# Hybrid decoder layer: value projection moved between features six and seven, half of the rotary sine multiplies on GpSimd, and a new written order

## The chip, the cores and the metric

The kernel runs on one core of a Trainium2 chip. The metric is the device time of one execution in microseconds; the time before is the median of three runs. The engines are TensorE (PE in the profile; its weight loads PEld), VectorE (DVE), ScalarE (ACT), GpSimd (POOL) and SyncE (SP), which issues most loads.

## The reference

One decoder layer for 512 positions of width 1024, in float32:

```python
proj = x @ w_in
rq, rk, rv, rg, aq, ak, av, iq, ik, iw = jnp.split(proj, IN_SPLITS, axis=-1)
...
# rotary embedding of rq, rk, aq, ak, iq, ik
return jnp.concatenate([x1 * cos - x2 * sin, x1 * sin + x2 * cos], axis=-1)
...
# retention, 4 heads, chunks of 128
scores = jnp.einsum('nbhid,nbhjd->nbhij', qc, kc) * decay_intra
inner = jnp.einsum('nbhij,nbhjd->nbhid', scores, vc)
...
# indexer: 8 heads score all earlier keys, the 128 best are kept per query
score = jnp.einsum('bqh,bqhs->bqs', wb, logits)
_, sel = lax.top_k(score, topk)
# sparse softmax attention over the kept keys, 4 heads of 128
```

The retention output is normalised per head and multiplied by silu(rg); both outputs go through one output projection, a residual and a layer norm, then a SwiGLU feed-forward part of width 2816 with its own residual and norm.

## The kernel before, in words

**Products.** The projections are taken as three matmuls in the rounded float32 format (`mm3`, lines L101 to L103): high times high, high times low, low times high. So each half of a weight tile (128 x 1024) must be *prepared*: a high part `wh` and a low part `wl = raw - wh`. The number behind `wh` and `wl` counts the halves in the order in which TensorE uses them. The string `HOW` says how each half is prepared. For `V`, ScalarE casts (L93) and VectorE subtracts (L98). For `Q` (`lower`, L733 and L734), ScalarE copies `-raw` rounded into `wl` and a DMA issued by GpSimd adds `raw` to it in place; TensorE may use it when that DMA has landed. `N` is ScalarE with a VectorE operation of two scalars. Raw tiles of 1 MB come by SyncE into three buffers (`raw`).

**Main stream.** `main()` yields groups of TensorE work in this order: the eight features `pf0` to `pf7` (two halves each, 24 matmuls a half; 0 and 1 are attention keys, 2 and 3 attention queries, 4 and 5 retention keys `rkT`, 6 and 7 retention queries `rqT`), the retention value `pt1` in two parts (48 matmuls each; the second part stands inside `proj_pair`), and `proj_pair`: the attention value and the gate `grg` by a Strassen-like scheme of seven products P1 to P7, in the banks `pa`, `pc` and `pb`. Sums of raw tiles that this scheme needs (B11 + B12 and so on) are made by DMAs that add DRAM data to a raw tile (`plus`, L208). Then the mixed output projection (`mx`).

**Rotation.** `rope` (L273 to L278) takes two half copies on ScalarE (`rt2`), a cosine multiply on VectorE (L275), a sine multiply on VectorE (L276) and an addition on GpSimd (L278, L411). The index queries and the index key are rotated too; their sums go into `qs` and `ks` on VectorE. A rotated attention key or query leaves by a DMA into `akT` or `aqT`.

**Order.** Nothing is scheduled automatically: each engine takes its instructions in program order, and that is written by hand in `PLAN`. Its words: `M` is the next group of the main stream, `k` the next step of the side work (index rotation, index logits `lg`, top-k), `w` prepares the next half, `f` fetches a raw tile; `S1` to `S4`, `P3`, `P5` to `P7` make the sides of the Strassen scheme, `a`, `b`, `c`, `d` its raw sums, `kt`, `sc`, `st`, `oa`, `ob`, `rs`, `rg`, `tu` the steps of retention (`rs` scores on TensorE, `ri` outputs, `rz` turned outputs), `g` the gate's silu, `as`, `t`, `p` those of attention, `kl` the low part of the attention key (`akl`). A step that waits on one engine holds everything behind it on that engine. The feed-forward part, from about 268 us on, has an order of its own.

Of the kernel before, what the change touches and what calls it, by code (L numbers as in the profile page):

```python
# [53 lines left out]
def hybrid_layer_kernel(ctx: ExitStack, tc: tile.TileContext, xT, x, pos, w0, wf, wt, wo,  # L54
# [181 lines left out]
    for kt in range(KT):  # L236
# [30 lines left out]
        if kt in (3, 5):  # L267
            next(tables_it)
    def rope(dst, src, ct, st, lo=0):
        t1 = tmp("rt1")  # L270
# [2 lines left out]
        A.copy(t2[0:64, n], src[64:128, n])  # L273
# [1 line left out]
        V.tensor_tensor(t1[:, n], src[:, n], ct[:, n], op=ALU.mult)  # L275
        V.tensor_tensor(t2[:, n], t2[:, n], st[:, n], op=ALU.mult)  # L276
# [130 lines left out]
    def put_feature(c, i, acc):  # L407
        dst = feats[c // 2][:, 2 * (c % 2) + i]
        if c < 4:
            t1, t2 = rope(None, acc, CT, ST)  # L410
            G.tensor_tensor(t1, t1, t2, op=ALU.add)  # L411
# [587 lines left out]
w f M k M M w M M M M M M w k f M M k k w k M k w k M M M k M M M w M k M k M k M k k k f w w M k k k M M k k k M k k k f k M k f k k k M k k k M w k  # L999
# [891 lines left out]
```

## Time and profile before

| | us |
|---|---|
| median of three runs (604.88 to 606.65) | 605.32 |
| the profiled execution | 605.22 |
| its span | 603.4 |
| TensorE busy | 593.0 (98%) |
| VectorE busy | 528.6 (88%) |
| ScalarE busy | 399.4 (66%) |
| GpSimd busy | 200.3 (33%) |
| DMA: accumulating and other GpSimd queue, share of 16 engines | 41.2% |
| DMA: SyncE's loads, share of 16 engines | 37.8% |

The granted clock is 1.00 in all stretches shown. A row of the time line gives start and duration in us, then engine, line, operation, output and inputs, and in brackets the engine's idle time before it with what ended it. A row of waits gives the total, the number of times and the longest.

### The profile page before, as it was taken

The page shows a single profiled execution, that of the slowest core. Times are in us where ns is not written, and L with a number is a line of the kernel's source. Part 1 is how long each engine was busy: PE and PEld are TensorE (multiplying, and loading weights), DVE is VectorE, ACT ScalarE, POOL GpSimd, SP SyncE. Part 2 cuts the span into 40 slices and gives each one's busy share as a digit, 9 for nine tenths or more (in the row PEclk, how much of TensorE's full clock was granted, in tenths as well). Part 3 has the DMA queues.
Part 4 walks back from the last instruction along what each step waited for, and adds up shares of the span by engine and source line. Part 5 has one row for each costly group of instructions (what it writes and reads, how often), then busy time and mean ns, then how long its engine had stood idle before and what let it go on. Part 6 is the DMA issues. An engine that isn't in the chain of part 4 may idle for free.

```text
span 603.4 us, 9333 instructions
## 1 busy us (share of the span) xinstructions
PE 593.0 (98%) x3205; PEld 513.6 (85%) x3205; DVE 528.6 (88%) x941; ACT 399.4 (66%) x701; POOL 200.3 (33%) x220
## 2 busy tenths in 40 slices
PE   8999999999999999999999999999999999999996
PEld 6987888888887788889998888888888888888885
DVE  5868889988889999889999898989898989799995
ACT  4588575653689877677758677777677756485701
POOL 0067523351448021242003444444443423331120
PEclk9999999999999999999999999999999999999999
DMA  8988729989989698797347888888888999999412
GB/s 265 267 226 232 272 92 256 241 195 239 160 183 243 202 255 360 211 225 142 88 143 191 179 207 171 206 166 205 168 208 179 198 272 223 225 201 275 130 53 87
DMA packets 53600, 121.27 MB, mean 201 GB/s; under 512 B 9217, under 2 KB 26177, under 8 KB 48049
## 3 DMA queue, kind: packets, MB, share of 16 engines
q0 software_dynamic: 26160, 43.20, 41.2%
q1 hardware_dynamic: 26800, 76.69, 37.8%
q10 hardware_dynamic: 592, 0.79, 0.4%
q8 instruction: 25, 0.41, 0.3%
q14 instruction: 23, 0.18, 0.1%
HBM read 83.43 MB, written 2.10 MB: 142 GB/s over the span
## 4 chain that ended last, share of the span: by engine, by line
PE 85%; DMA 6%; POOL 3%; DVE 2%; issue 2%; SPq 2%; ACT 1%; POOLq 0%; ACTq 0%
PE ga L1098 17%; PE gc L1098 8%; PE gb L1098 4%; PE ga L1111 4%; PE pf L103 3%; PE pf L102 3%; PE pf L101 3%; DMA wl<-raw 3%; PE mx L101 2%; PE mx L103 2%; PE mx L102 2%; PE dl L101 2%; PE dl L103 2%; PE dl L102 2%; PE gc L1111 2%; DMA w0s<-in_w_dram 2%
## 5 line engine op out<-in xcount | busy, mean ns | idle before, releaser
L1051 POOL DMA_DIRECT2D t<-t x36 | 30.8, 856 | 80.7 <-DVE t L1151 48.5
L103 PE MATMUL pf<-xh,wl 128*128 128x512 f32 x128 | 50.1, 391 | 0.7 <-DMA wl<-raw 0.7
L98 DVE TENSOR_TENSOR wl<-raw,wh 128x1024 fp32r<-128x1024 f32 x34 | 42.6, 1258 | 9.0 <-ACT wh L93 8.9
L101 PE MATMUL pf<-xh,wh 128*128 128x512 f32 x128 | 50.0, 391 | 0.0
L102 PE MATMUL pf<-xl,wh 128*128 128x512 f32 x128 | 49.9, 390 | 0.0
L1051 POOL DMA_DIRECT2D w<-w x36 | 31.7, 1026 | 41.7 <-DVE w L1137 38.2
L93 ACT CAST wh<-raw 128x1024 fp32r<-128x1024 f32 x34 | 35.7, 1052 | 13.1 <-PE pt L103 4.2
L603 POOL TENSOR_TENSOR rs<-ve,half 128x1 f32<-128x1 f32 (+1 forms) x10 | 12.3, 1230 | 52.0 <-DVE ve L602 52.0
L103 PEld LDWEIGHTS pf<-xh,wl 128*128 128x128 f32 x128 | 24.0, 188 | 6.5 <-DMA wl<-raw 1.5
L102 PEld LDWEIGHTS pf<-xl,wh 128*128 128x128 f32 x128 | 24.1, 188 | 4.7
L101 PEld LDWEIGHTS pf<-xh,wh 128*128 128x128 f32 x128 | 24.0, 188 | 4.7
L580 DVE MAX8 m<-score 128x8 f32<-128x256 f32 (+2 forms) x48 | 26.7, 557 | 0.7
L581 DVE MATCH_REPLACE8 score<-m,score 128x256 f32<-128x256 f32 (+2 forms) x48 | 26.0, 543 | 0.0
L1066 POOL DMA_DIRECT2D graw<-graw x17 | 25.9, 1521 | 0.4 <-ACT graw L1065 0.4
L1200 ACT COPY t<-ga 128x512 f32<-128x512 f32 x17 | 10.0, 588 | 23.8 <-PE ga L1098 23.8
L734 POOL DMA_DIRECT2D wl<-raw x14 | 12.9, 920 | 31.9 <-ACT wl L733 29.0
L93 ACT CAST dhp<-sum 128x1024 fp32r<-128x1024 f32 x12 | 12.6, 1053 | 15.4 <-PE dl L103 5.8
L1168 ACT COPY w<-ga 128x512 f32<-128x512 f32 x18 | 10.6, 587 | 12.7 <-PE ga L1098 12.7
L276 DVE TENSOR_TENSOR rt<-rt,tables 128x512 f32<-128x512 f32 (+1 forms) x21 | 18.9, 902 | 0.0
L101 PE MATMUL dx<-dhp,slot 128*128 128x512 f32 x48 | 18.7, 389 | 0.0
L102 PE MATMUL dx<-dlp,slot 128*128 128x512 f32 x48 | 18.7, 389 | 0.0
L103 PE MATMUL dx<-dhp,slot 128*128 128x512 f32 x48 | 18.7, 389 | 0.0
(1237 smaller groups left out, 2103.7 us busy)
## 6 DMA issues: line engine op xcount, KB each, us to landing
graw<-in_wgu_dram SPq DMA_DIRECT2D x22, 1024.0 KB, 5.1
raw<-in_wo_dram SPq DMA_DIRECT2D x8, 1024.0 KB, 5.7
raw<-in_wf_dram SPq DMA_DIRECT2D x7, 1024.0 KB, 5.9
wl<-raw POOLq DMA_DIRECT2D x14, 512.0 KB, 8.3
raw<-in_wt_dram SPq DMA_DIRECT2D x6, 1024.0 KB, 6.5
r<-in_wd_dram SPq DMA_DIRECT2D x12, 512.0 KB, 6.2
w<-w POOLq DMA_DIRECT2D x36, 128.0 KB, 3.1
t<-t POOLq DMA_DIRECT2D x36, 128.0 KB, 4.9
```

The lines of the kernel that those rows point to most:

```text
L93: A.copy(hi, src)
L98: eng_lo.tensor_tensor(lo, src, hi.bitcast(F32), op=ALU.subtract)
L101: T.matmul(acc, lhsT=lh, rhs=rh, start=first, stop=False, **kw)
L102: T.matmul(acc, lhsT=lh, rhs=rl, start=False, stop=False, **kw)
L103: T.matmul(acc, lhsT=ll, rhs=rh, start=False, stop=last, **kw)
L276: V.tensor_tensor(t2[:, n], t2[:, n], st[:, n], op=ALU.mult)
L580: V.max(m8, a)
L581: V.match_replace(out=a, in_to_replace=m8, in_values=a, imm_value=TAKEN)
L1051: nc.gpsimd.dma_start(t[:, :Q], t[:, Q:], accum_op=ALU.add)
L1066: nc.gpsimd.dma_start(u[:, :S], u[:, S:], accum_op=ALU.add)
L1098: T.matmul(full[:, :Q] if low else full, lhsT=w[:, i * S + k * P:i * S + k * P + P], rhs=rhs, start=first and not low and k == 0, stop=las ...
L1111: T.matmul(gp[n][acc], lhsT=a[:, i * S + k * P:i * S + k * P + P], rhs=parts[q][:, k, b], start=first and j == 0, stop=j == 11, skip_group ...
```

## The change

1. The value projection is no longer cut in two: all 96 of its matmuls stand between features 5 and 6, so features 6 and 7 come right before P1. The weights follow (`stream`, `wanted`).
2. `SINES` sends 11 of the 21 sine multiplies to GpSimd; `ADDS` sends 4 of the 16 additions from GpSimd to VectorE.
3. `SUMS` makes two of the six raw sums (half 1 of B11 + B12 and of B12 + B22) on VectorE from tiles that are loaded.
4. `HOW` has 18 entries `Q` in the place of 14: halves 3 to 7, 9, 13, 16, 18, 19, 27, 28, 32, 33, 37, 38, 42, 43; before, 3, 4, 5, 11, 12, 13, 15, 25, 27, 28, 32, 33, 37, 39.
5. The second block's gate multiply of retention goes from VectorE to GpSimd. The strings in `gate` and `ret_score` name GpSimd throughout, as before.
6. `proj_pair` calls `settle()`, which issues the pending evacuation, after each t.
7. `PLAN` is written anew.

```diff
-    stream = [wf[c] for c in range(8)] + [wt[1, i] for i in range(2)]
+    stream = [wf[c] for c in range(6)] + [wt[1, i] for i in range(2)] + [wf[c] for c in (6, 7)]
...
+    SUMS = dict(zip(((B11, B12), (B11, B22), (B12, B22), (B11, B21)), "DV DD DV DD".split()))
...
     def plus(a, b, i):
+        if SUMS[a, b][i] == "V":
+            V.tensor_tensor(raws[a][:, i], raws[a][:, i], raws[b][:, i], op=ALU.add)
+            return
...
-    HOW = "VVVQQQVVVVVQQQVQVVVVVVVVVQVQQVNNQQVVVQVQVVVVVVVVV"
+    HOW = "VVVQQQQQVQVVVQVVQVQQVVVVVVVQQVNNQQVVVQQVVVQQVVVVV"
...
+    SINES = iter("GGVVVVVVVGGGGVGGVVGGG")
+    ADDS = iter("VGGGGGGGVVGVGGGG")
...
-        V.tensor_tensor(t2[:, n], t2[:, n], st[:, n], op=ALU.mult)
+        (G if next(SINES) == "G" else V).tensor_tensor(t2[:, n], t2[:, n], st[:, n], op=ALU.mult)
...
-        for c in (2 * part, 2 * part + 1):
+        for c in range(4):
...
-            if q == "P5":
-                yield from proj_value(1)
...
+                    settle()
...
-        (G if b > 1 else V).tensor_tensor(tok[1][:, b], tok[1][:, b], tok[2][:, b], op=ALU.mult)
+        (G if "VGGG"[b] == "G" else V).tensor_tensor(tok[1][:, b], tok[1][:, b], tok[2][:, b], op=ALU.mult)
...
-        for c in range(8):
+        for c in range(6):
             yield from proj_feature(c)
-        yield from proj_value(0)
+        yield from proj_value()
+        for c in (6, 7):
+            yield from proj_feature(c)
         yield from proj_pair()
...
-w f M k M M w M M M M M M w k f M M k k w k M k w k M M M k M M M w M k M k M k M k k k f w w M k k k M M k k k M k k k f k M k f k k k M k k k M w k
+w M M k M w M M f M M w M k f M M k k M w k k M w k M f k M k M M w M M k k k M k M M w f M w k f k k k k M k k k M k k k M k k k w k k M k k M k k k
```

Lines of the changed kernel are numbered 4 to 11 higher than those of the same statements before (L734 is L738, L276 is L284, L411 is L419).

GpSimd from the clearing of `kk` on, at about 31 us, before: `wl3` is the first lowered half; `rt` are rotation tiles, `ql` and `qa` index queries.

```order
L293 MEMSET kk3_309 128x1024
L734 DMA wl3_407<-raw1_263 128x1024
L411 ISA
L411 TENSOR_TENSOR rt1_415<-rt1_415,rt2_416 128x512
L412 DMA akT_313<-rt1_415 128x512
L411 TENSOR_TENSOR rt1_447<-rt1_447,rt2_448 128x512
L412 DMA akT_313<-rt1_447 128x512
L734 DMA wl4_477<-raw2_265 128x1024
```

The same place after:

```order
L301 MEMSET kk3_309 128x1024
L284 ISA
L284 TENSOR_TENSOR rt2_391<-rt2_391,tables_117 128x384
L738 DMA wl3_405<-raw1_263 128x1024
L284 TENSOR_TENSOR rt2_414<-rt2_414,tables_117 128x512
L420 DMA akT_313<-rt1_413 128x512
L419 TENSOR_TENSOR rt1_447<-rt1_447,rt2_448 128x512
L420 DMA akT_313<-rt1_447 128x512
L738 DMA wl4_462<-raw2_265 128x1024
```

The sine multiply of the first index query has moved ahead of half 3, and the first key's addition has become a sine multiply.

GpSimd a little later, from half 5 on, after only (before, halves 6 and 7 were subtracted on VectorE and the rows `wl6` and `wl7` were not there, the others stood in the same order):

```order
L738 DMA wl6_567<-raw3_436 128x1024
L315 TENSOR_TENSOR ql_308<-qs_558,qa_306 128x384
L320 DMA qa_306<-ql_308 32x768 x2
L320 DMA qb_307<-ql_308 32x768 x2
L419 TENSOR_TENSOR rt1_582<-rt1_582,rt2_583 128x512
L420 DMA akT_313<-rt1_582 128x512
L419 TENSOR_TENSOR rt1_625<-rt1_625,rt2_626 128x512
L420 DMA akT_313<-rt1_625 128x512
L738 DMA wl7_649<-raw3_436 128x1024
```

Half 6 has come in ahead of the last index query's transfers, and half 7 behind the keys' last addition and transfer.

ScalarE around 180 us, before: `akl` is the low part of the attention key, `wl32` the low half that TensorE's `pb` waits for, `grg` the gate.

```order
L733 ACTIVATE akl_1773<-akT_313 128x1024
L653 ACTIVATE rstate2_1783<-rstate1_1672,cols_79 128x128 x4
L499 ACT_TABLE_LOAD
L499 ACTIVATE grg_1665<-grg_1665 128x512
L358 ACTIVATE wh31_1809<-raw10_1169 128x1024
L733 ACTIVATE akl_1773<-akT_313 128x1024
L733 ACTIVATE wl32_1822<-raw13_1776 128x1024
```

The same place after:

```order
L737 ACTIVATE akl_1768<-akT_313 128x1024
L657 ACTIVATE rstate2_1794<-rstate1_1675,cols_79 128x128 x4
L737 ACTIVATE akl_1768<-akT_313 128x1024
L366 ACTIVATE wh31_1808<-raw10_1237 128x1024
L504 ACT_TABLE_LOAD
L504 ACTIVATE grg_1650<-grg_1650 128x512
L737 ACTIVATE wl32_1824<-raw13_1713 128x1024
```

The second half of `akl` and `wh31` have moved ahead of the table load and the gate; the same steps stand ahead of `wl32`.

More of the change, by code (lines that the diff above doesn't have):

```diff
@@ L211, in plain @@
         return lambda i: raws[c][:, i]
-    HOW = "VVVQQQVVVVVQQQVQVVVVVVVVVQVQQVNNQQVVVQVQVVVVVVVVV"
-    wanted = [*range(8), 8, B11, 9, B11, B11, B12, B22, B11, B21, *range(B21 + 1, len(stream))]
+    HOW = "VVVQQQQQVQVVVQVVQVQQVVVVVVVQQVNNQQVVVQQVVVQQVVVVV"
+    wanted = [*range(B11), B11, B11, B11, B12, B22, B11, B21, *range(B21 + 1, len(stream))]
     entries = [(plain(c), i, HOW[2 * n + i] if 2 * n + i < len(HOW) else "V") for n, c in enumerate(wanted) for i in range(2)]
@@ L275, in rope @@
         V.tensor_tensor(t1[:, n], src[:, n], ct[:, n], op=ALU.mult)
-        V.tensor_tensor(t2[:, n], t2[:, n], st[:, n], op=ALU.mult)
+        (G if next(SINES) == "G" else V).tensor_tensor(t2[:, n], t2[:, n], st[:, n], op=ALU.mult)
         if dst is not None:
-            G.tensor_tensor(dst, t1[:, n], t2[:, n], op=ALU.add)
+            (G if next(ADDS) == "G" else V).tensor_tensor(dst, t1[:, n], t2[:, n], op=ALU.add)
         return t1, t2
@@ L410, in put_feature @@
             t1, t2 = rope(None, acc, CT, ST)
-            G.tensor_tensor(t1, t1, t2, op=ALU.add)
+            (G if next(ADDS) == "G" else V).tensor_tensor(t1, t1, t2, op=ALU.add)
             nc.gpsimd.dma_start(dst, t1)
@@ L438, in hybrid_layer_kernel, with proj_value @@
     tok = {}
-    value = []
-    def proj_value(part):
+    def proj_value():
         def evac(b):
@@ L447, in evac @@
             A.copy(tok[1][:, b, :KV], value[b])
-        if part == 0:
-            value.extend(psu(f"pt1_{b}")[:, :KV] for b in range(NB))
-        for c in (2 * part, 2 * part + 1):
+        value = [psu(f"pt1_{b}")[:, :KV] for b in range(NB)]
+        for c in range(4):
             h, l = weight()
@@ L499, in gate @@
         A.activation(tok[2][:, b], tok[2][:, b], AF.Silu)
-        G.tensor_tensor(tok[2][:, b], tok[2][:, b], gnb, op=ALU.mult)
+        (G if "GGGG"[b] == "G" else V).tensor_tensor(tok[2][:, b], tok[2][:, b], gnb, op=ALU.mult)
     def proj_pair():
@@ L627, in ret_score @@
             rt["q", b] = tmp(f"rqd{b}")
-            G.tensor_tensor(heads(rt["q", b]), rqT[:, :, bs], heads(rt["decay"][:, 1]), op=ALU.mult)
+            (G if "VGGG"[b] == "G" else V).tensor_tensor(heads(rt["q", b]), rqT[:, :, bs], heads(rt["decay"][:, 1]), op=ALU.mult)
         sc = psu(f"rs{b}")
@@ L998, in hybrid_layer_kernel @@
     PLAN = """
[L999 to L1005 removed]
+w M M k M w M M f M M w M k f M M k k M w k k M w k M f M k M M M w M M k k k M k M M w f M w k f k k k k M k k k M k k k M k k k w k k M k k M k k k
+M w k k f k M k w M M M k x k S1 k M M w M k k k w M S3 M M M S2 k k k w k k M k M k M M M M P7 P5 w f M w M M M M S4 M w M kf k k k f k k f k M M w M
+k M M w a0 k k c0 M P6 M M k M f y w k k a1 M M w b0 k M M c1 k M w k M k M M M kt0 kt2 k w k M k b1 z ql sc1 d0 sc0 st0 M k w M kt1 d1 w M w oa0 ob0
+M M k w oa1 rs0 k M ob1 st1 M M M k P3 rs1 f k sc2 k w M M w oa2 sc3 kl0 ob2 st2 M kl1 w g3 M k w g2 rs2 oa3 M ob3 M as0 rg2 w g0 rq M f g1 k f rs3 k
+M as0 rg1 rg0 k k M rg3 as0 tu2 M tu0 f w M M tu3 gl0 w t00 ra0 M M t01 sq t02 M ra1 t03 M tu1 as1 w k M M M w as1 as1 M M M k M t10 p00 t11 al M as2
+p10 k w p11 ga0 M M t12 gl1 k t13 rq3 M mx w M M p01 p02 p03 p12 k p13 k M M M as2 as3 M M as2 w lg w M ga1 M w t20 M as3 M M t21 M w M p20 as3 t22
+t30 t31 M M p21 t23 ga2 M su0 M p22 M su1 w M p30 en1 p23 en0 p31 M M t32 M M M M M w M ga3 M w M e00 e01 M t33 w p32 e10 M p33 w M e11 M M
 """
```

6 lines of the change are left out of this document (removed).

## The prediction

> **What bounds the kernel now.** I read the page first, then TensorE's busy time in stretches of 20 us, then its list of waits, and last the time line around each wait.
>
> From the page: the span, and the busy time of the engines.
>
> ```profile
> span 603.4 us, 9333 instructions
> PE 593.0 (98%) x3205; PEld 513.6 (85%) x3205; DVE 528.6 (88%) x941; ACT 399.4 (66%) x701; POOL 200.3 (33%) x220
> ```
>
> TensorE works 593.0 of 603.4 us. The matmuls are the same before and after, so the change can only move the 10.4 us in which it does not work. The stretches say where these are (columns: PE, PEld, DVE, ACT, POOL busy, clock, DMA share, GB/s):
>
> ```profile
> core 0: us, PE busy (x) PEld busy (x) DVE busy (x) ACT busy (x) POOL busy (x), PEclk, DMA share, GB/s
> ...
> 40.00:60.00 20.00, 19.34 (x87) 15.40 (x86) 16.41 (x20) 17.37 (x33) 15.70 (x22) 1.00 0.93 256
> 60.00:80.00 20.00, 20.00 (x99) 17.14 (x98) 16.70 (x28) 10.80 (x24) 8.64 (x9) 1.00 0.61 224
> ...
> 180.00:200.00 20.00, 17.67 (x96) 14.64 (x95) 18.81 (x49) 19.94 (x38) 13.90 (x13) 1.00 0.91 211
> 200.00:220.00 20.00, 20.00 (x115) 17.37 (x114) 19.30 (x47) 16.17 (x31) 3.05 (x3) 1.00 0.85 235
> ```
>
> Between 20 and 260 us, the part that the change rewrites, only two stretches have idle TensorE: 0.66 us at 40:60 and 2.33 us at 180:200, together 2.99. The list of waits puts names to them:
>
> ```profile
> PE pb L102 <- DMA wl<-raw: 1.4, 1, 1.4
> PE fin L1820 <- ACT diag L1819: 1.3, 1, 1.3
> PE acc L257 <- ACT w0h L248: 1.2, 1, 1.2
> PE warm L222 <- PEq L1880: 0.8, 1, 0.8
> PE as L754 <- DVE mx L758: 0.7, 1, 0.7
> PE pf L103 <- DMA wl<-raw: 0.7, 2, 0.4
> PE pc L101 <- DVE grg L526: 0.2, 1, 0.2
> ```
>
> Rows `fin`, `acc` and `warm` lie at the two ends of the program, which the change leaves alone. The reachable ones are 1.4 + 0.7 + 0.7 + 0.2 = 3.0 us, and 2.1 of them are a lowered half (`wl`, finished by a GpSimd DMA) that lands too late. The best that the change can do is thus 605.2 - 3.0 = 602.2; what it can lose has no such limit, and that is the shape of this forecast. All sums stand on the profiled execution (605.22 us, span 603.4), 0.1 under the median of 605.32.
>
> **The prices.** First the kinds of work that change engine (min/median/max ns of one, or us for the landing, where three are given):
>
> ```profile
> L98 DVE TENSOR_TENSOR wl<-raw,wh 128x1024 fp32r<-128x1024 f32 x34 | 42.6, 1258 | 9.0 <-ACT wh L93 8.9
> L276 DVE TENSOR_TENSOR rt<-rt,tables x21: 549/681/2559, 35.5 to 127.8; 128x512 f32<-128x512 f32 x17, 128x384 f32<-128x384 f32 x4
> L411 POOL TENSOR_TENSOR rt<-rt,rt x8: 1285/1300/1960, 38.6 to 83.0; 128x512 f32<-128x512 f32 x8
> L734 POOL DMA_DIRECT2D wl<-raw x14: 860/879/1235, 35.3 to 215.6; - x14
> DMA to landing us min/median/max: 4.7/8.3/11.0
> ```
>
> VectorE: four subtracts fewer (-4 x 1.26), eleven sines fewer (-11 x 0.68), four additions more (4 x 0.68, as the sine), two 128x1024 sums more (2 x 1.26, as the subtract), one gate multiply fewer (-0.68): -8.0 us. GpSimd: eleven sines, minus four additions, plus one gate, each 1.30: +10.4; four more lowering DMAs minus two accumulating ones, at 0.88: +1.8; together +12.2. ScalarE: an entry that goes from V to Q adds one activation, 1.04 in a row below: 4 x 1.04 = +4.2. None of these is TensorE time. VectorE and GpSimd have room on average; these sums become time only where a queue's delay reaches TensorE, so I go through the places where it can. Two of the six accumulating DMAs leaving the queues frees transfer time that I count at nothing.
>
> A measure that serves for all lowered halves: in the written order I count the TensorE rows between the point where a half is issued and its first use. Two 128x512 matmuls start 0.23 us apart:
>
> ```profile
> 192.30 0.39 PE L102 MATMUL pa<-wl,xh 128*128 128x512 f32 x1
> 192.53 0.39 PE L103 MATMUL pa<-wh,xl 128*128 128x512 f32 x1
> ```
>
> In these units, from before to after: half 3 goes 11.1 to 5.7 us, 4 from 5.7 to 6.1, 5 from 3.9 to 4.1, 6 from 12.2 to 5.7, 7 from 14.2 to 4.5, 32 from 9.2 to 10.6, 37 from 6.4 to 8.6, 38 from 4.0 to 8.4; on VectorE, 40 from 10.3 to 2.1 and 41 from 2.5 to 1.9.
>
> **Early, 35 to 72 us: +0.5.** Half 3 is what TensorE first waits for. The rows: VectorE's first rotary multiply, issue and landing of half 3, then issue, landing time and first use of half 4; below them GpSimd's last key transfer and the use of half 7.
>
> ```profile
> 34.98 0.56 DVE L275 TENSOR_TENSOR rt<-acc,tables 128x384 f32<-128x384 f32 x1 [0.84 <-ACT wl L733]
> 35.26 0.95 POOL L734 DMA_DIRECT2D wl<-raw  x1 [2.81 <-ACT wl L733]
> wl<-raw POOLq DMA_DIRECT2D x1, 512.0 KB, 10.2
> 42.94 0.94 POOL L734 DMA_DIRECT2D wl<-raw  x1
> wl<-raw POOLq DMA_DIRECT2D x1, 512.0 KB, 6.2
> 51.55 0.40 PE L103 MATMUL pf<-xh,wl 128*128 128x512 f32 x1
> ...
> 63.01 0.56 POOL L412 DMA_DIRECT2D akT<-rt  x1 [0.30 <-POOL rt L411]
> 70.64 0.39 PE L103 MATMUL pf<-xh,wl 128*128 128x512 f32 x1
> ```
>
> Half 3 was issued at 35.26 and landed at 45.46, and TensorE waited up to 0.4 for it. Now the sine multiply of the first query stands ahead of that issue on GpSimd. It needs the same tables as VectorE's multiply at 34.98, so it starts no earlier; a 128x384 operation on GpSimd costs between 0.56 (VectorE's row) and 1.30, so the issue comes at 35.5 to 36.3, at most 1.0 later. If the landing follows in full, 1.0 is added; if the transfer is paced by the queues that it shares (DMA share 0.93 in the stretch above), nothing is. I take the middle, +0.5, since the 10.2 us are far over the 6.2 of half 4 and so mostly sharing. Behind the sine on GpSimd nothing else is in a hurry: half 4 waits for a raw tile and is issued as before.
>
> Half 4 landed at 49.14 and was used at 51.55: with 5.7 of written lead it was 2.4 early; half 5 with 3.9 was up to 0.4 late (row `pf`). Halves 6 and 7 are new on this path. Number 6 has 5.7, as half 4 had: 2.4 early, so 0. Number 7 is the thin one. On GpSimd it now follows the second `akT` transfer, which before was done at 63.01 + 0.56 = 63.6; half 6's issue, 0.9, lies ahead of that as well: issued at 64.5, used at 70.64, a lead of 6.1. At the latency of half 4, 6.2, it is just in time; at the least, 4.7, it is 1.4 early; at the median, 8.3, 2.2 late; at the worst, 11.0, 4.9 late. I take half 4's, since the stretch 60:80 has a DMA share of 0.61 against 0.93 in the one where half 3 took 10.2, and cost it at 0; what a late half 3 adds, half 7 is needed later. Ends for this part: -0.3 (half 3 unhurt and one of the two waits gone) and +4.9.
>
> **The middle, 70 to 165: 0.** Here the order of work changes most, but leads are 8 to 15 us. The new tight place is the query's rotation: feature 7 now ends right before P1, and the first retention scores follow 30 matmuls of 0.23 and two sets of four transposes (about 0.9) later, 7.8 us. One rotation takes two ScalarE copies, a VectorE multiply and two GpSimd operations:
>
> ```profile
> L273 ACT COPY rt<-pf x16: 584/586/587, 35.9 to 126.0; 64x512 f32<-64x512 f32 x16
> ```
>
> 2 x 0.59 + 0.68 + 2 x 1.30 = 4.5, which leaves 3.3 for whatever stands ahead of the multiply on VectorE: a weight's subtract (1.26) and a max with its replacement. That fits, so 0; ends 0 and +2.
>
> **180 to 200 us: -1.4.** The long wait, with its chain: ScalarE's copy of half 32, GpSimd's issue, the landing time, and TensorE's use.
>
> ```profile
> 184.71 1.04 ACT L733 ACTIVATE wl<-raw 128x1024 fp32r<-128x1024 f32 x1
> 186.04 0.86 POOL L734 DMA_DIRECT2D wl<-raw  x1
> wl<-raw POOLq DMA_DIRECT2D x1, 512.0 KB, 11.0
> 197.10 0.50 PE L102 MATMUL pb<-wl,xh 128*128 128x512 f32 x1 [1.45 <-DMA wl<-raw]
> ```
>
> ScalarE, 19.94 of 20 busy, sets the copy's time. In the new order the written lead of half 32 grows by 1.4 (0.4 of it more matmul rows ahead of its use), as large as the wait. The same ScalarE steps stand ahead of it in both orders (the rows are shown with the change), but the second `akl` copy comes two steps sooner, and its transfer is further on when half 32 starts. So -1.3 for the wait, and -0.1 for the slow first matmul behind it (0.50 against 0.39); ends 0 and -1.45.
>
> `as`, 0.7: the fourth score tile still reuses the first one's bank, and VectorE still reaches the reading late, with top-k steps and two subtracts in its queue: 0; ends -0.7 and +0.7 (twice the row). `pc`, 0.2: the subtract it waits for stands a little earlier: -0.1.
>
> **200 to 262: 0.** Weight 38 becomes lowered, among the loads of the output weights. Its nearest row is that of weight 39, lowered before, V now:
>
> ```profile
> 215.61 0.87 POOL L734 DMA_DIRECT2D wl<-raw  x1 [1.53 <-ACT wl L733]
> wl<-raw POOLq DMA_DIRECT2D x1, 512.0 KB, 10.6
> 228.29 0.39 PE L102 MATMUL mx<-wl,mah 128*128 128x512 f32 x1
> ```
>
> 39 landed at 226.21, 2.1 before its use, with a written lead of 8.4. Weight 38 gets 8.4 too: 2 early, 0. Weights 40 and 41 are left with 2.1 and 1.9 on VectorE for a 1.26 subtract behind a cast: 0.7 to spare, no wait unless VectorE is late. Ends 0 and +1.5.
>
> **Sum:** 605.2 + 0.5 + 0 - 1.4 - 0.1 + 0 = 604.2.
>
> [...] One pair of rows in the time line, with the page's group of the same multiply, shows GpSimd and VectorE standing in each other's way:
>
> ```profile
> 43.52 2.34 POOL L307 TENSOR_TENSOR ql<-qs,qa 128x384 fp32r<-128x384 f32 x2
> 43.73 2.56 DVE L276 TENSOR_TENSOR rt<-rt,tables 128x384 f32<-128x384 f32 x1
> ...
> L276 DVE TENSOR_TENSOR rt<-rt,tables 128x512 f32<-128x512 f32 (+1 forms) x21 | 18.9, 902 | 0.0
> ```
>
> VectorE's sine multiply took 2.56 us beside two GpSimd operations, against a least of 0.55; over all 21 the mean is 0.90 and the median 0.68, so most are not hit, but one hit is as long as the neighbour. [...]
>
> **The rivals.**
>
> 1. *Faster: all of 180 to 200 goes and nothing is lost early.* For it: half 3's latency is mostly sharing, and VectorE has 8 us less to do, so it may read the first `as` tile sooner. Against: that tile's place on VectorE is behind the same top-k steps. 605.2 - 1.45 - 0.7 - 0.2 + 0 to 0.5 early: 602.9 to 603.4.
>
> 2. *Slower: half 7 lands late.* One mechanism: it goes to GpSimd's queue behind half 6, four query DMAs, two additions and two `akT` DMAs, and then shares the DMA engines with these and a raw tile. It decides at the point where the wait eats what is gained later (1.5) and 1.8 more, 3.3 late, a latency of 6.1 + 3.3 = 9.4. At the 10.2 of half 3: 605.2 + 4.1 - 1.5 = 607.8. For it: that row; against: the emptier queues of 60:80.
>
> 3. *GpSimd's extra operations hold VectorE back.* Eight more GpSimd tensor operations; if each blocks one VectorE operation for its 1.30, VectorE gets 10.4 more and 8.0 less, 2.4 more work instead of 8.0 less. It reaches TensorE at `as` and `pc`, which wait for VectorE today: one block of 1.3 on each. 604.2 + 2.6 = 606.8. For it: the pair above; against: the median of 0.68 beside a mean of 0.90, most operations are not hit.
>
> 4. *The gain is handed on.* TensorE comes 1.4 sooner to weights 40 and 41, whose 0.7 to spare is eaten, and gets the rest back as a wait there: 604.2 + 0.7 = 604.9, no change.
>
> **How the numbers follow.** A difference under 0.3% (1.8 us) can't be told from none here; so faster means under 603.5, slower over 607.1. The forecast's own case, 603.5 to 604.9: 0.38. The first rival: 0.37, as three separate waits of 1.4, 0.7 and 0.2 can shrink, and an early loss need not come. The second: 0.16. The third: 0.06, of which 0.04 over 607.1, since its price is a least one. The fourth: 0.03. So faster 0.37, no change 0.38 + 0.03 + 0.02 = 0.43, slower 0.16 + 0.04 = 0.20. Predicted is the forecast's sum, 604.2. The range goes from 602.0 (all 3.0 of the reachable waits, with 0.2 of slow matmuls behind them) to 607.8 (half 7 at half 3's latency): left out are the tail of the second and third rivals, about 0.1, and some 0.05 below.
>
> **What the profile after would show.** Right: `pb <- DMA wl` gone or under 0.3 and 180:200 near 19 us of TensorE; `pf <- DMA wl` between 0.7 and 1.7 in one or two early waits; `as <- DVE` about 0.7; no `mx` among the waits; VectorE some 6 to 8 us less busy, GpSimd about 12 us more, TensorE's 593 unchanged. Wrong in the first direction: a third and fourth `pf` wait (halves 6, 7). In the second: `as`, `rs` or `mx` waiting for VectorE, with its multiplies well over 0.68 beside GpSimd rows. The forecast falls if half 32 is late still: then its landing, not ScalarE's place for it, set the wait.

## The result and the profile after

| | us |
|---|---|
| the changed kernel, median of 7 runs (608.72 to 611.72) | 609.46 |
| the kernel before, median of 7 runs (604.76 to 608.61) | 606.02 |
| ratio, with its 95% interval | 1.0057 (1.0035 to 1.0080) |
| profiled execution, span: after | 609.52, 607.7 |

The change made the kernel slower by 0.57%, about 3.4 us. From the page of the changed kernel:

```profile
PE 595.0 (98%) x3205; PEld 513.9 (85%) x3205; DVE 525.9 (87%) x931; ACT 402.6 (66%) x705; POOL 212.5 (35%) x230
```

The work moved about as counted: GpSimd +12.2, ScalarE +3.2, VectorE only -2.7 in the place of -8.0 us. TensorE's idle time is 12.7 us in the place of 10.4. Its busy time is also 2.0 longer with the same matmuls; the largest parts are those of `ri` (+0.8) and `as` (+0.5), which wait now, and of `acc` at the start (+0.5). The first matmul behind the waits of `pf` and `mx` has a row of 0.50 against 0.39 (that of `mx` is below), and the one behind the longest wait of `ri` 0.38 against 0.28, but that is not all of it: a kernel below without most of these waits (e6) still has 593.8. TensorE's waits (sum, count, longest):

```profile
PE ri L665 <- DVE rst L637: 1.7, 2, 1.5
...
PE mx L102 <- DMA wl<-raw: 1.3, 1, 1.3
PE pf L103 <- DMA wl<-raw: 1.1, 2, 0.7
...
PE rz L697 <- DVE rv L689: 0.6, 1, 0.6
PE ri L667 <- DVE rstate L658: 0.6, 1, 0.6
PE as L101 <- DVE mrl L618: 0.6, 1, 0.6
PE as L758 <- DVE mx L762: 0.4, 1, 0.4
PE as L101 <- ACT apts L783: 0.3, 1, 0.3
```

The stretches from 160 us on, with the columns of the prediction's windows:

```profile
160.00:180.00 20.00, 18.34 (x106) 15.22 (x105) 19.23 (x46) 15.06 (x26) 8.22 (x8) 1.00 0.92 193
180.00:200.00 20.00, 18.37 (x105) 15.48 (x105) 19.57 (x52) 17.86 (x31) 14.83 (x13) 1.00 0.85 210
200.00:220.00 20.00, 19.11 (x105) 16.27 (x104) 18.09 (x49) 17.21 (x37) 3.06 (x3) 1.00 0.86 251
220.00:240.00 20.00, 18.72 (x104) 15.70 (x103) 17.52 (x35) 16.22 (x32) 1.68 (x2) 1.00 1.02 344
```

The wait that the forecast wanted gone, `pb` for half 32 (1.4 us), is gone, and `pc` with it. In its place stand six waits of the same part of the program that were not there: `ri` for `rst` 1.7, `ri` for `rstate` 0.6, `rz` 0.6, `as` 0.6 and 0.3, `mx` 1.3, together 5.1 us, and `pf` has 0.4 more. Five of the six are at retention and attention, and by the profile VectorE ends four of them and ScalarE one. Two places in the time line show why. First VectorE and GpSimd around 173 us:

```profile
173.11 3.22 DVE L683 SCALAR_TENSOR_TENSOR nmr<-mv,rs 128x4 f32<-128x4 f32 x1
177.64 0.68 DVE L637 TENSOR_TENSOR rst<-rs,both 128x512 f32<-128x512 f32 x1
...
173.45 2.86 POOL L632 TENSOR_TENSOR rqd<-rqT,both 128x512 f32<-128x512 f32 x2
```

`nmr` is an operation on 128x4 numbers, part of the retention scale. It took 3.22 us and ended at 176.33, as GpSimd's two multiplies of 128x512 did (176.31). `rst`, which `ri` waits for, is behind it on VectorE. The second place is at 194 us, with ScalarE's next step:

```profile
194.31 2.12 DVE L683 SCALAR_TENSOR_TENSOR nmr<-mv,rs 128x4 f32<-128x4 f32 x1
...
193.58 2.82 POOL L505 TENSOR_TENSOR grg<-grg,gnb 128x512 f32<-128x512 f32 x2
...
196.47 1.51 ACT L686 ACTIVATE rv<-ri,nmr,rs 128x128 f32<-128x128 f32 x4 [2.08 <-DVE nmr L683]
```

Again the small operation ends with GpSimd's pair (196.43 and 196.40), and ScalarE stands still for 2.08 us. In the order before, the retention scale of block 3 (`rs3`) stood ahead of these two gate multiplies (`g0`, `g1`); in the new one it stands behind them. The decayed queries `rqd` were on GpSimd before as well, but two of them never stood in a row beside `nmr`. Neither pair is made of the sines that the change moved. The wait of `ri` for `rstate` (0.6, at 185.2) is no such meeting: VectorE's operations ahead of it, from 182 us on, have no GpSimd tensor operation beside them until 185.15. Its cause was not isolated.

The last new wait is half 38, now lowered. ScalarE's copies of attention weights ahead of it, GpSimd's issue and TensorE's use, in the time line:

```profile
215.24 0.82 ACT L783 COPY apts<-apt 128x256 f32<-128x256 f32 x2 [1.62 <-PE apt L781]
217.31 0.85 POOL L738 DMA_DIRECT2D wl<-raw  x1 [5.42 <-ACT wl L737]
...
227.01 0.50 PE L102 MATMUL mx<-wl,mah 128*128 128x512 f32 x1 [1.28 <-DMA wl<-raw]
```

The list of transfers has it with its size and the time from issue to landing:

```profile
wl<-raw POOLq DMA_DIRECT2D x1, 512.0 KB, 9.7
```

It was issued at 217.31 and landed 9.7 later; TensorE was there 1.28 us early.

### The profile page after: what moved, and what is told of

Read it like the earlier page. It is cut to its first block, busy times and chain, and to the rows that moved or that the text cites. A ratio compares the mean times of both kernels' runs of the same rounds, so it can differ in the third digit from the quotient of the medians.

```text
span 607.7 us, 9332 instructions
## 1 busy us (share of the span) xinstructions
PE 595.0 (98%) x3205; PEld 513.9 (85%) x3205; DVE 525.9 (87%) x931; ACT 402.6 (66%) x705; POOL 212.5 (35%) x230
## 4 chain that ended last, share of the span: by engine, by line
PE 74%; DVE 8%; DMA 6%; issue 4%; POOL 4%; ACT 4%; ACTq 0%; SPq 0%; POOLq 0%; DVEq 0%
PE ga L1104 17%; PE gc L1104 8%; PE gb L1104 4%; PE ga L1117 4%; DMA wl<-raw 3%; PE pf L103 3%; PE pf L101 2%; PE pf L102 2%; PE dl L102 2%; PE dl L101 2%; PE dl L103 2%; DVE wl L98 2%; PE gc L1117 2%; PE mx L102 2%; PE mx L103 2%
## 5 line engine op out<-in xcount | busy, mean ns | idle before, releaser
L98 DVE TENSOR_TENSOR wl<-raw,wh 128x1024 fp32r<-128x1024 f32 x30 | 40.1, 1344 | 14.1 <-ACT wh L93 13.8
L101 PE MATMUL pf<-xh,wh 128*128 128x512 f32 x128 | 50.0, 390 | 0.0
L93 ACT CAST wh<-raw 128x1024 fp32r<-128x1024 f32 x30 | 31.5, 1056 | 21.9 <-DMA raw<-in_wt_dram 8.1
L738 POOL DMA_DIRECT2D wl<-raw x18 | 16.7, 927 | 42.5 <-ACT wl L737 18.8
L101 PEld LDWEIGHTS pf<-xh,wh 128*128 128x128 f32 x128 | 24.0, 188 | 4.8
L284 POOL TENSOR_TENSOR rt<-rt,tables 128x512 f32<-128x512 f32 (+1 forms) x11 | 15.9, 1447 | 22.1 <-ACT rt L282 19.6
L93 ACT CAST dhp<-sum 128x1024 fp32r<-128x1024 f32 x12 | 12.7, 1055 | 15.7 <-DMA sum<-in_wd_dram 5.2
L737 ACT ACTIVATE wl<-raw 128x1024 fp32r<-128x1024 f32 x18 | 19.1, 1063 | 1.9 <-PE mx L102 1.6
L607 POOL TENSOR_TENSOR rs<-ve,half 128x1 f32<-128x1 f32 (+1 forms) x10 | 10.7, 1069 | 26.3 <-DVE ve L606 26.1
L1174 ACT COPY w<-ga 128x512 f32<-128x512 f32 x18 | 10.6, 588 | 12.7 <-PE ga L1104 12.7
L372 ACT CAST wh<-raw 128x1024 fp32r<-128x1024 f32 x18 | 18.7, 1042 | 0.0
L101 PE MATMUL dx<-dhp,slot 128*128 128x512 f32 x48 | 18.7, 389 | 0.0
```

Source lines behind the costliest of these rows:

```text
L93: A.copy(hi, src)
L98: eng_lo.tensor_tensor(lo, src, hi.bitcast(F32), op=ALU.subtract)
L101: T.matmul(acc, lhsT=lh, rhs=rh, start=first, stop=False, **kw)
L737: A.activation(dst, src, AF.Copy, scale=-1.0)
```

## The experiments

Theory A: a VectorE operation that comes up beside a GpSimd tensor operation is held until GpSimd is through (the two `nmr` rows above, 3.22 and 2.12 us, end within 0.03 us of GpSimd's pair), and the new order puts such meetings on the paths that TensorE waits for. Rival B: VectorE simply has too much work in 140 to 200 us (19.2 to 19.7 of 20 busy). Rival C: the lowered half 38 is a loss of its own. Rival D: the sines on GpSimd are the harm. All times are medians; the kernel before, run beside each, is given with its own. It moved from 604.77 to 606.25 between the rounds, and the changed kernel ran only in the first (ratio 1.0057). So "less than the changed kernel" below is given twice: by the plain medians, and by the difference of the ratios, which takes out that movement. Single ratios carry an interval of 1 to 2 us to each side.

**e1: two decayed queries back on VectorE.**

```diff
-            (G if "VGGG"[b] == "G" else V).tensor_tensor(heads(rt["q", b]), ...
+            (G if "VGVV"[b] == "G" else V).tensor_tensor(heads(rt["q", b]), ...
```

> The changed kernel, with the decayed retention queries of blocks 2 and 3 (two 128x512 multiplies back to back on GpSimd, 2.86 us at 173.45) made on VectorE. Theory A, exclusion: the 128x4 operation nmr that took 3.22 us on VectorE at 173.11 was held by these two; it falls under 0.7 us, the wait of ri for rst (1.5 us) falls under 0.3, and the span goes from 607.7 to about 606.3, although VectorE gets 1.4 us more to do. Theory B, VectorE has simply too much work between 140 and 180 us (19.2 to 19.7 of 20 us busy): with 1.4 us more the wait grows to nearly 3 us and the span to about 609.

Measured: 607.67 (before 605.66; ratio 1.0034, 1.0017 to 1.0051), 1.8 less than the changed kernel by the medians, 1.4 by the ratios; the intervals of the two overlap a little. VectorE's `nmr` at the same place in the time line:

```profile
172.57 0.16 DVE L683 SCALAR_TENSOR_TENSOR nmr<-mv,rs 128x4 f32<-128x4 f32 x1
```

One of TensorE's waits:

```profile
PE ri L665 <- DVE rst L637: 0.2, 1, 0.2
```

With 1.4 us more work on VectorE, `nmr` fell from 3.22 to 0.16 and the wait of `ri` from 1.7 to 0.2. That is theory A, and B is out for this wait. `mx` took back 0.4 (1.7 in the place of 1.3).

**e2: the retention scale of block 3 ahead of the gates.**

```diff
-... ob3 M as0 rg2 w g0 rq M f g1 k f rs3 k
+... ob3 M as0 rg2 w rs3 g0 rq M f g1 k f k
```

> The changed kernel, with the retention scale of block 3 (rs3) written ahead of the gate steps g0 and g1, as the order before had it; no engine's work changes. Theory A: nmr at 194.31, 2.12 us beside two gate multiplies on GpSimd, falls under 0.7; ScalarE's wait of 2.08 for it goes, and with it most of the waits rz (0.6), as (0.6 and 0.3) and part of mx (1.3): 1.5 to 2.8 us less. Theory B: VectorE has the same work in the same stretch, so no change beyond 0.5 us. Theory C, the lowered half 38 is late by itself: rz and as may shrink, but mx keeps 1.3 us or takes over what the others give up, and the span stays within 1 us.

Measured: 609.13 (before 605.66; ratio 1.0064, 1.0040 to 1.0088): no gain that can be told in the time (by the ratios 0.4 more than the changed kernel), a miss for theory A's number. But the wait moved as expected. The time line, and TensorE's longest wait:

```profile
192.82 0.15 DVE L683 SCALAR_TENSOR_TENSOR nmr<-mv,rs 128x4 f32<-128x4 f32 x1
```

```profile
PE mx L102 <- DMA wl<-raw: 1.7, 1, 1.7
```

`nmr` went from 2.12 to 0.15, `rz` is not among the waits, the two `as` waits at L101 lost 0.5 together; `mx` grew from 1.3 to 1.7. The mechanism is A's, and part of what it frees goes to the wait behind it, as theory C had it, with the time within 1 us.

**e3: both.**

> Both of the two edits above together. Theory A: the gains add, 3 to 4.3 us less than the changed kernel, 603.4 to 604.7 of span, no slower than the kernel before. Theory B: slower than the second edit alone by 1 us or more. If the gains do not add, the first one is given back as a wait of mx for its lowered half.

Measured: 607.84 (before 605.66; ratio 1.0020, 0.9992 to 1.0049), single runs from 603.62 to 609.88: not to be told from e1 alone. Theory A's sum (a span of 603.4 to 604.7) was a miss, at 606.9. In the profiled execution (608.74) the wait of `mx` is longer:

```profile
PE mx L102 <- DMA wl<-raw: 2.0, 1, 2.0
```

The stretches of 1 us behind it show why that costs more than 2.0 (third column from the right: the granted clock):

```profile
225.00:226.00 1.00, 1.00 (x5) 0.81 (x4) 0.00 (x0) 1.00 (x2) 0.00 (x0) 0.70 0.99 406
226.00:227.00 1.00, 1.00 (x4) 0.81 (x3) 0.00 (x0) 1.00 (x2) 0.00 (x0) 0.50 1.05 430
227.00:228.00 1.00, 1.00 (x4) 0.71 (x4) 0.22 (x1) 0.50 (x1) 0.00 (x0) 0.50 1.01 414
228.00:229.00 1.00, 1.00 (x4) 0.81 (x3) 0.48 (x2) 0.00 (x0) 0.00 (x0) 0.59 1.10 442
```

After the wait TensorE's clock is at half: 0.30 + 0.50 + 0.50 + 0.41 = 1.7 us of full speed lost in these 4 us, in which TensorE was busy throughout.

**e4: the new order with the engine choices of before** (sines on VectorE, additions on GpSimd, raw sums by DMA, the gate multiply of block 1 on VectorE):

```diff
-    SINES = iter("GGVVVVVVVGGGGVGGVVGGG")
-    ADDS = iter("VGGGGGGGVVGVGGGG")
+    SINES = iter("V" * 21)
+    ADDS = iter("G" * 16)
...
-    SUMS = dict(zip(..., "DV DD DV DD".split()))
+    SUMS = dict(zip(..., "DD DD DD DD".split()))
...
-        (G if "VGGG"[b] == "G" else V).tensor_tensor(tok[1][:, b], ...
+        (G if "VVGG"[b] == "G" else V).tensor_tensor(tok[1][:, b], ...
```

(The raw sums are eight halves: eight such DMAs are in the trace of the kernel before and here, six in the changed kernel. The list of changes and the forecast count six in the kernel before.)

> The changed kernel's order and lowered set, but with the engine choices of before: all sines on VectorE, all rotation additions on GpSimd, all raw sums by DMA, the gate multiply of block 1 on VectorE. Theory A as seen in the trace (the two collisions come from work that GpSimd had before too, only placed otherwise): the waits ri<-rst and rz stay, and the span is within 1.5 us of 607.7. Theory D, the sines that moved to GpSimd are what holds VectorE: L98 and nmr go back to their 1.26 and 0.43 us mean, the waits behind 160 us go and the span returns to 603.5 to 605.5. Theory B: VectorE has 5 us more, span 609 or more.

Measured: 614.85 (before 605.66; ratio 1.0157, 1.0123 to 1.0191), 5.4 over the changed kernel. Its two longest waits:

```profile
PE rs L635 <- POOL rqT L286: 3.2, 1, 3.2
PE rz L697 <- DVE rv L689: 2.2, 1, 2.2
```

The span did not return to 603.5 to 605.5 (it is 614.1), so rival D's number failed, and so did A's (within 1.5; the wait of `ri` for `rst` is not in the list either). B's number, 609 or more, came, but not for B's reason: VectorE stood idle just ahead of the longest wait. GpSimd's issue of one raw sum, its landing, VectorE's next operation, and the addition that `rs` waits for:

```profile
141.30 0.88 POOL L213 DMA_DIRECT2D raw<-in_wt_dram  x1
raw<-in_wt_dram POOLq DMA_DIRECT2D x1, 512.0 KB, 11.3
...
153.83 1.23 DVE L98 TENSOR_TENSOR wl<-raw,wh 128x1024 fp32r<-128x1024 f32 x1 [6.35 <-ACT wh L93]
...
157.53 1.26 POOL L286 TENSOR_TENSOR rqT<-rt,rt 128x512 f32<-128x512 f32 x1 [8.92 <-DVE rt L284]
```

The raw sum landed at 152.6. ScalarE's cast of that half began at 152.75 (the profile puts its wait down to a matmul of `pa` that ended at 152.74, but its queue's wait ended at 152.67, with the landing). VectorE waited 6.35 us for the cast, and the rotation's last sine (156.70) stands behind that on VectorE. In the changed kernel VectorE makes this sum itself at 142.22, in 1.22 us. So the 3.2 us of `rs` come from the raw sum's way back to a DMA, not from sines on VectorE. The 2.2 us of `rz` end with VectorE's two gate multiplies (2.35 us from 201.25), beside one on GpSimd. Behind each of the two waits the clock falls (0.97 and 0.69 in the 5 us from 155 and from 160, 0.91 and 0.75 in those from 200 and from 205), 1.7 us of full speed lost each time. What the sines alone are worth in this order, e4 does not tell; it changes four things at once, and only b1 moves the rotation by itself.

**e5: half 38 on VectorE.** In `HOW`, entry 38 from `Q` to `V`.

> The changed kernel, with weight half 38 prepared on VectorE (V) and not lowered by a DMA (Q); nothing else. Theory C, its late landing is a loss of its own: the wait of mx for wl (1.3 us in the changed kernel, 1.7 in the two edits before) goes, nothing takes its place, and the time falls by 1.3 to 1.9 us, to about 607.8. Theory B, VectorE is full: its subtract of 1.22 us near 218 us makes mx or as wait for VectorE instead and the time stays within 0.5 us.

Measured: 607.75 (before 604.97; ratio 1.0045, 1.0028 to 1.0062), 1.7 less than the changed kernel by the medians, but 0.7 by the ratios, and the intervals overlap. The time alone does not decide; the list does: no wait of `mx`, and nothing longer than 0.3 (`lg`) that is new. That speaks for theory C: this wait is a loss of its own, and VectorE could take the subtract.

**e6: e1, e2 and e5 together.**

> The three edits together: rqd of blocks 2 and 3 on VectorE, rs3 ahead of the gates, half 38 on VectorE. Where the two edits without half 38 were profiled, mx waited 2.0 us, the granted clock then fell to 0.5 for about 3 us and that cost some 1.6 us more; single runs of it lie between 603.6 and 609.9. Theory E, that spread is the clock's answer to a wait of about 2 us: without the wait the time is 603.0 to 605.0 with single runs within 2.5 us of each other. Rival: the spread is the chip's, runs still differ by 5 us or more, and the median is over 605.5.

Measured: 604.81 (before 604.97; ratio 0.9994, 0.9976 to 1.0012), single runs from 604.19 to 606.25, a width of 2.1 where e3 had 6.3. All of TensorE's waits but `fin` and `warm`:

```profile
PE pf L103 <- DMA wl<-raw: 0.8, 1, 0.8
PE ri L667 <- DVE rstate L658: 0.5, 1, 0.5
PE as L758 <- DVE mx L762: 0.5, 1, 0.5
PE as L101 <- DVE mrl L618: 0.4, 1, 0.4
```

The stretch from 160 us, for comparison with the one of the changed kernel:

```profile
160.00:180.00 20.00, 19.98 (x123) 17.58 (x124) 19.23 (x49) 16.80 (x31) 6.51 (x7) 1.00 0.90 204
```

VectorE is as busy there as in the changed kernel (19.23) and TensorE works 19.98 in the place of 18.34 us: rival B is out for this stretch. Three edits that touch two multiplies, one place in the order and one half take back the whole loss: 4.7 us by the medians, 3.8 by the ratios, and here the intervals (0.9976 to 1.0012 against 1.0035 to 1.0080) lie apart. That is more than e1, e2 and e5 give apart (1.7 together by the ratios, 3.8 by the medians), as where a wait handed on has a lower clock behind it (0.50 behind the 2.0 us in e3); but the single intervals leave that open. The width of 2.1 us is as theory E had it. Whether waits near 2 us are all that spreads the runs is not shown: the kernel before, whose longest wait in its profile is 1.4, spread from 602.98 to 608.63 in the same round.

**e7: the value projection split again, the rest as changed** (`proj_value(0)` behind feature 7 and `proj_value(1)` behind P1, stream and `HOW` reordered with the tiles).

> The changed kernel with the value projection split as before (its first half behind feature 7, the second behind P1), the weights' ways of preparation carried along with their tiles, the engine moves and the written order kept. It tells what the move of the value does. If features 6 and 7 at the new place are what crowds VectorE between 140 and 180 us (rotation, sums and top-k together), VectorE is under 19 of 20 us there, the waits of ri for rst go, and the time is 606 to 608. If the written order alone places the collisions, the waits stay and the time is within 1 us of 609.5; it can also be slower, since that order was written for the other sequence.

Measured: 621.65 (before 604.97; ratio 1.0273, 1.0242 to 1.0303). TensorE's longest wait:

```profile
PE pt L102 <- DMA wl<-raw: 4.6, 1, 4.6
```

The granted clock is 0.50 in the 5 us behind it. The order does not fit the other sequence, so this says nothing on what the move of the value costs by itself. It stays open: each sequence needs an order of its own.

**b1: the kernel before with the rotation's new engine choices alone.**

> The kernel before, with the engine choices of the rotation alone taken from the changed kernel: 11 sine multiplies on GpSimd, 4 additions on VectorE. Theory A: exclusion costs only where a collision stands on a path that TensorE waits for; before 160 us VectorE's leads are long in this order, so the time is within 1 us of the kernel before (605.0 to 606.7). Theory D, the sines on GpSimd are the harm: rotated tiles come later and VectorE is held, 607 or more.

Measured: 604.39 (before 604.97; ratio 0.9991, 0.9972 to 1.0009). No change, as A said, and `pb` waits 1.4 as before. The rotation's new engines neither gain nor lose in the old order, and rival D is out there. They do cost VectorE something that TensorE does not see: the mean subtract goes from 1.26 to 1.32 us.

**b2: the kernel before with `rs3` late**, where the new order has it.

```diff
-... rg2 g3 w rs3 M f g0 g1 M k as0
+... rg2 g3 w M f g0 g1 M k as0 rs3
```

> The kernel before, with one step moved: the retention scale of block 3 (rs3) stands behind the gate steps g0, g1 and the first score step, where the changed order has it, instead of ahead of them. Theory A: nmr now comes up on VectorE while GpSimd does two gate multiplies in a row (192.5 to 195.0 us), takes 1.3 us or more instead of 0.15, ScalarE waits for it, rz waits 0.5 us or more for VectorE, and the time is 0.5 to 2 us longer. Theory B: the same VectorE work in the same stretch, so nmr stays under 0.5 and the time within 0.5 us.

Measured: 607.11 (before 604.77; ratio 1.0035, 1.0012 to 1.0058), 2.3 more. The meeting happened, but it hit the operation just ahead of `nmr`, on the row's maximum of the first scores (time line):

```profile
191.95 2.92 DVE L760 TENSOR_SCALAR mx<-mx 128x4 f32<-128x4 f32 x1
...
192.04 2.79 POOL L500 TENSOR_TENSOR grg<-grg,gnb 128x512 f32<-128x512 f32 x2
```

TensorE's wait for half 32, and the stretch behind it:

```profile
PE pb L102 <- DMA wl<-raw: 2.4, 1, 2.4
```

```profile
195.00:200.00 5.00, 2.64 (x10) 2.12 (x10) 4.83 (x12) 4.97 (x14) 1.27 (x1) 0.78 0.77 152
```

The expected duration for `nmr` was a miss (0.15). The small operation that came up there was held, as A said, for 2.92 us; in the kernel before the same operation took 1.21. But this did not make the time: there is no `rz` wait, and no wait for `mx`. The `as` wait (0.7) went, TensorE came to `pb` sooner and waits 2.4 there instead of 1.4, and the clock behind it falls (0.78 in this stretch, 0.88 in the next 5 us), 1.7 us of full speed lost. So b2 shows the meeting, and that a wait which goes can cost more than it did; it does not show the meeting's price.

**b3: b1 with half 32 on VectorE.** In `HOW` of the kernel before, entry 32 from `Q` to `V`.

> The kernel before, with the rotation's engine choices of the changed kernel, and half 32 prepared on VectorE. If the wait of pb (1.4 us), the one gain that the changed order did bring, is the late start of a lowering on a full ScalarE, one activation and one transfer fewer there end it without a new order: pb's wait goes or falls under 0.3, and the time is 602.8 to 603.6 beside 604.97 of the kernel before. If VectorE (18.8 of 20 us busy there) can't take 1.22 us more, as or pc wait longer by as much and the time does not move.

Measured: 604.88 (before 604.77; ratio 0.9998, 0.9984 to 1.0012). `pb` is gone from the list, and the same `as` wait as before has grown from 0.7 to 2.0:

```profile
PE as L757 <- DVE mx L761: 2.0, 1, 2.0
```

So the 1.4 us of `pb` are worth nothing here as long as VectorE, which got the subtract, is late for `as`.

**e8: e6 with two more edits** (block 1's decayed query on VectorE, `st2` ahead of `ob2`).

> The three edits, and two more of the same kind: block 1's decayed query on VectorE too (GpSimd's multiply at 155.4 us stands beside a subtract of 2.66 us), and the retention state st2 written ahead of ob2, so that VectorE adds it before the statistics of ri2. Theory A: the subtract falls to 1.3, the wait of ri for rst (0.35) and the one for rstate (0.5) go, and the time falls by 0.6 to 1.2 us, to about 603.8. Theory B: VectorE's 0.68 more near 155 us eats it, no change within 0.4.

Measured: 608.87 (before 604.77; ratio 1.0068, 1.0047 to 1.0089), 4.1 more than e6 (4.5 by the ratios), a miss for both theories. The waits of `ri` went, as expected, but earlier VectorE work made a new meeting: `nmr` came up at 184.24 against two gate multiplies with a DMA issue between them. The time line, and the wait that follows from it:

```profile
184.24 3.93 DVE L683 SCALAR_TENSOR_TENSOR nmr<-mv,rs 128x4 f32<-128x4 f32 x1
...
184.42 1.59 POOL L505 TENSOR_TENSOR grg<-grg,gnb 128x512 f32<-128x512 f32 x1
186.26 1.88 POOL L505 TENSOR_TENSOR grg<-grg,gnb 128x512 f32<-128x512 f32 x1
```

```profile
PE as L758 <- ACT rv L686: 3.6, 1, 3.6
```

Behind it the clock is 0.66 in the 5 us from 190, 1.7 us of full speed lost: 3.6 and 1.7 us are more than the loss.

**e9: one of the two decayed queries on VectorE** (`"VGVG"` in e1's line).

> The changed kernel with one of the two decayed queries (block 2) on VectorE, so that GpSimd does one multiply in place of two in a row near 173.5 us. If VectorE is let in between two GpSimd operations, two in a row held it no longer than one would: nmr stays near its 3.2 us less nothing, or the wait of ri does not change. If it is held until the row of GpSimd operations is over, nmr now takes at most one of them, 0.2 to 1.5 us, the wait of ri for rst falls from 1.5 to under 0.5, and the time falls by 1 to 1.6 us, as with both moved (607.7).

Measured: 610.35 (before 606.25; ratio 1.0077, 1.0047 to 1.0107). The time line, and the wait for half 38:

```profile
172.99 1.98 DVE L683 SCALAR_TENSOR_TENSOR nmr<-mv,rs 128x4 f32<-128x4 f32 x1
...
173.32 1.61 POOL L632 TENSOR_TENSOR rqd<-rqT,both 128x512 f32<-128x512 f32 x1
```

```profile
PE mx L102 <- DMA wl<-raw: 1.8, 1, 1.8
```

`nmr` takes 1.98 with one neighbour (0.2 to 1.5 was expected), 3.22 with two, 0.16 with none. So it was held through both of GpSimd's multiplies in the changed kernel. That is not so for every two in a row. In the kernel before, `nmr` of block 3 met two and went in between them:

```profile
188.83 1.26 DVE L679 SCALAR_TENSOR_TENSOR nmr<-mv,rs 128x4 f32<-128x4 f32 x1 [0.46 <-POOL rs L603]
...
188.78 1.28 POOL L685 TENSOR_TENSOR rv<-rv,grg 128x512 f32<-128x512 f32 x1
190.04 1.27 POOL L500 TENSOR_TENSOR grg<-grg,gnb 128x512 f32<-128x512 f32 x1
```

It ended at 190.09, as the first GpSimd operation did (190.06). One difference between the rows: here the second GpSimd row begins 0.03 us ahead of the first one's end, while the two `rqd` rows of the changed kernel (1.62 us each, 2.86 together) overlap by 0.38.

The wait of `ri` fell from 1.7 to 1.0, less than expected. The time did not fall at all: `mx` waits 1.8 in the place of 1.3, and the clock is 0.81 in the 5 us from 225 and 0.85 in the next 5, 1.7 us of full speed lost.

## Why the prediction was wrong

The forecast's sum, minus 1.0 us, met a span that grew by 4.3 (603.4 to 607.7) in the profiled executions. By stretch, TensorE's idle time in us, before and after:

| stretch | forecast | idle before | idle after | change |
|---|---|---|---|---|
| 0 to 20 | 0 | 1.98 | 0.78 | -1.2 |
| 20 to 70 | +0.5 | 0.66 | 1.08 | +0.4 |
| 70 to 160 | 0 | 0 | 0 | 0 |
| 160 to 180 | no term from 165 on | 0 | 1.66 | +1.7 |
| 180 to 200 | -1.5 | 2.33 | 1.63 | -0.7 |
| 200 to 262 | 0 | 0 | 2.17 | +2.2 |
| TensorE's busy time | 0 | 593.0 (busy) | 595.0 (busy) | +2.0 |

The steps that failed are the stretch from 165 us to 180, for which the sum has no term, the 0 for 200 to 262, and the busy time taken as unchanged; the first 20 us hid a part of it by luck.

- **165 to 180, no term: the step that failed first.** The working goes from "the middle, 70 to 165" to "180 to 200", on the ground that VectorE and GpSimd "have room on average" and that it goes "through the places where it can" reach TensorE. The wait of `ri` for `rst` (1.5 of its 1.7 us, at 177 to 178.6) lies between. It comes from `nmr`, held 3.22 us by two GpSimd multiplies; e1 took them away and the wait went. Taking each operation at its median (0.15 for `nmr`) leaves no place for such a meeting. The third rival had this mechanism, at 0.06 and with the wrong meeting places: it counted GpSimd's *new* operations, while the meetings that cost were with old ones (`rqd`, `grg`) in a new order. What should have been read are the rows of the two orders side by side: which VectorE operations with a path to TensorE stand beside GpSimd operations.
- **The middle, 0: right.** TensorE was idle 0.2 us in it (at 160.8, counted in the row 160 to 180). The rotation's chain left 0.4 us to spare: the addition ended at 153.60, and the first `rs` matmul that needs it, the seventh (in e4 six ran ahead of the wait), began at 154.03.
- **VectorE, -8.0: missed, -2.7.** `nmr` went from a mean of 0.43 to 1.46 over its four executions (+4.1), the 30 subtracts from 1.26 to 1.34 (+2.6), the two raw sums took 1.59 each; against that the sines gave 10.4 and not 7.5. The longer subtracts come with the rotation's new engines, by b1 (1.32) and e4 (1.27); no wait of TensorE followed from them in b1.
- **180 to 200: right for the two waits it names, not for the stretch.** `pb` and `pc` left the list, and for the reason given: half 32 was issued 11.2 us ahead of its use (1.0 of them TensorE's own waits) in the place of 9.6, and landed in 8.5 in the place of 11.0. But `ri` for `rstate` (0.6) and `rz` (0.6) came in. That the gain would be handed on was the fourth rival, at 0.03 and 0.7 us; b3 shows the same for a wait ended by another route.
- **"As" 0, right for the wait it means:** 0.4 after against 0.7, both at the first scores. The two `as` waits at L101 belong to the next stretch.
- **Early, +0.5: right in size, by luck.** `pf` waits 1.1 against 0.7. But GpSimd's sine did not delay half 3; it started ahead of the estimate, and the issue stayed at 35.27:

```profile
34.31 1.02 POOL L284 TENSOR_TENSOR rt<-rt,tables 128x384 f32<-128x384 f32 x1 [2.46 <-DMA tables<-trig]
```

  TensorE came earlier instead: the wait of `acc` at the start (1.2 us) is not in the list after. That wait belongs to the execution and not to the change: it is 0.5 in b3, 0.6 in e1, 0.9 in e3, 1.0 in e4 and not listed in b1, b2 or e2. Half 7, the slower rival's mechanism, was not late: the two `pf` waits are those of halves 3 and 5.
- **200 to 262, 0: failed by 2.2 us.** Two waits of `as` at L101 (0.9 together) and `mx` (1.3). For `mx` the step was to give half 38 the spare time of half 39, because both have a written lead of 8.4. But 39 was issued 12.7 us ahead of its use (215.61 to 228.29), 4.3 more than is written, and 38 just the 8.4 (217.31, wanted at 227.01 - 1.28): ScalarE's copy for 38 stands behind `apts` copies that wait for TensorE (1.62), so it can't run ahead of TensorE's rows. The 8.4 against the 10.6 of the row that the forecast used would have said 2.2 late; with the 9.7 that it took, it was 1.3.
- **What a wait costs.** The sum took each at its length and TensorE's 593 as fixed. In the changed kernel busy time grew by 2.0 besides. And the wait of 2.0 us in e3 cost nearly as much again, by the clock (1.7 us of full speed).

## What to carry to other kernels

Price a reorder by meetings, not by totals: for every small VectorE operation that leads to TensorE, look at what GpSimd does at that moment in the new order, and allow for what `nmr` showed here: 3.22 us beside two GpSimd multiplies in the place of 0.16, ended with the second (in the kernel before 1.26, ended with the first). Go through the whole span for this: a stretch that the sum skips is a term of 0. A lead counted in TensorE's rows holds only for an engine that runs free of TensorE; where its queue waits for TensorE's own results, the lead is what the rows behind that wait leave (8.4 us for half 38 here, 12.7 for half 39 before). Where one wait goes, ask what the next one was sheltered from: e2, e9, b2 and b3 each ended or shortened a wait and gained nothing that can be told, while the three edits together gave 3.8 us by the ratios.
